# A hybrid mLSTM and GLA decoder step: three column tiles at the head, constants and state traffic on GpSimd's queue, gate rows spread by DMA

## The chip, the cores and the metric

The kernel runs on one core of one Trainium2 chip. The metric is the device time of one execution in microseconds (us). The engines are TensorE (PE; PEld is its weight load), VectorE (DVE), ScalarE (ACT), GpSimd (POOL) and SyncE (SP). SP only issues DMAs here; POOL issues DMAs and does a little arithmetic.

## The reference

One decoder layer is computed for 256 prompt positions and 8 single-token samples, so every matrix product has 264 columns on the moving side (T = 264).

```python
p = x @ w_in                                   # 2048 -> 12312 columns, split into 13 segments
qk = silu(causal_conv(p.qk)); q, k = split(qk) # mLSTM branch
h = mlstm(q, k, v, itil, logf, C, n, m)        # chunkwise, running-max stabiliser m
ya = headnorm(h) * sigmoid(p.o) * silu(p.z)
o = gla(gq, gk, gv, logsigmoid(p.g @ w_gate_up + b) / 16, S)
yb = rmsnorm(o) * silu(p.bz)
merged = sigmoid(p.ga) * (ya @ w_pa) + sigmoid(p.gb) * (yb @ w_pb)
out = layernorm(ALPHA * x + merged @ w_out)
```

Outputs are the new activations of prompt and samples and the new states (C, n, m, conv rows, S) of both. All is float32.

## The kernel before

**Tiles of columns.** `units()` lists 129 column tiles of 128 outputs in a fixed order: 16 qk, one small tile (the gates), 8 av, 4 bq, 4 bk, 8 bv, 16 ao and az, 8 bz, 32 ga and gb, 16 pab, 16 out. For each tile `parts` (L212) runs 16 k slices. A float32 product is made of three fp32r matmuls: weights are split into `hi` (ACT, L203) and `lo` (DVE, L204), x into `xh` and `xl` (`split`, L208), and the slices give hi*xh (L223), hi*xl (L224) and lo*xh (L227). Weights come in pieces of 8 slices, 512 KB each (`load_raw`, L169, on SP's queue), four raw buffers, five buffers each of `hi` and `lo`. So TensorE eats a piece in 24 matmuls.

**Head.** Two tiles (HU = 2) run together at the start, by quarters of x: a quarter of x (528 KB), then a 256 KB weight piece for each of the two tiles, and so on (L1110 to L1118). Behind it come the constants par and cst on SP (L1122, L1123), and six more at tile 4 (L1148).

**Side work.** The rest is written as generators, which `pump` advances by a budget after each tile. PE's order is that of the program (`MANUAL`); DVE, ACT, POOL and SP are ordered by the framework's scheduler when the kernel is built, and each runs its queue strictly in that order. The side work touched here:
- `g_gates` (L280): rows m and u (16 x 264) are split into fp32r halves and spread over 128 partitions by matmuls with a selector `selr`: eight for `dmx` (L377, L378) and, in `g_a_prompt`, four for each head (L423).
- `g_a_decode` (L492): the samples' mLSTM states, 16 chunks `cch` of 512 KB. A chunk is loaded (L526), scaled by ACT (L555), updated by DVE (L571, L573) and stored by POOL (L564). Rows `kb` and `qb` are spread by DMA through `spread_rows` (L486). Loads and spreads go on SP's queue, stores on POOL's.
- `g_gla_prompt` (L678): seven levels of a block recursion; at levels 0 to 4 each of 8 pairs of head and half takes two matmuls with 64 columns (L707) and one masked copy (L730).
- `g_gla_decode` (L771): 8 state chunks `sch` (L778) and the spread rows `ga`, `gk`, `gq` on SP's queue, stores `sS` on POOL's.
- `g_ln_rows` (L940): four loads for the final norm, on SP's queue.

Of the kernel before, what the change touches and what calls it, by code (L numbers as in the profile page):

```python
# [13 lines left out]
F32 = mybir.dt.float32  # L14
# [7 lines left out]
L = 256  # L22
# [3 lines left out]
H = 4  # L26
# [21 lines left out]
HU = 2  # L48
# [35 lines left out]
def body(ctx, tc, xT, wbig, wsmall, par, cmask, lmask, sel, rowc, gate, wgu, cT, sT, nst, cst, lnr,  # L84
# [57 lines left out]
    one_c = const.tile([128, 1], F32, name="one_c")  # L142

# [13 lines left out]
    pieces = [(u, k, KH, u) for k in range(0, KT, KH) for u in range(HU)]  # L157
# [28 lines left out]
    def cast_piece():  # L186
        i = nxt["cast"]
        while nxt["dma"] <= i:
            load_raw()
        n, k, m, bi = pieces[i]  # L190
        nxt["cast"] += 1
        r = raws.pop(i)
        h = whi_p.tile([128, KR, 128], F32R, tag="hi", name="hi")[:, 0:m]
        if bi is None:
            w = SMALL
            A.copy(out=h[:, :, 0:w], in_=r)
            V.tensor_tensor(out=h[:, :, w:2 * w], in0=r, in1=f(h[:, :, 0:w]), op=ALU.subtract)
            for q in range(m):
                his[n, k + q] = h[:, q, 0:2 * w]
            return  # L200
        lo = wlo_p.tile([128, KR, 128], F32R, tag="lo", name="lo")[:, 0:m]
        with tc.high_priority(offset=PRIO):
            A.copy(out=h, in_=r)  # L203
            V.tensor_tensor(out=lo, in0=r, in1=f(h), op=ALU.subtract)  # L204
        for q in range(m):
            his[n, k + q], los[n, k + q] = h[:, q], lo[:, q]
# [5 lines left out]
    def parts(n, k0, k1, rhs, base=0):  # L212

        small = UN[n][0] == "small"
        m = 2 * SMALL if small else 128
        ps = ps_m.tile([128, 512], F32, tag="mm", name="mm")
        out = ps[0:m, 0:T]
        for k in range(k0, k1):
# [8 lines left out]
            PE.matmul(out, lhsT=los[n, k], rhs=rh, start=False, stop=(k == k1 - 1))  # L227
# [9 lines left out]
    st, sel_t = {}, {}  # L237
# [41 lines left out]

    def g_gates(ps):  # L280
# [36 lines left out]
        gr = lambda n: tmp.tile([16, T], F32R, tag="t1", name=n, bufs=T1_BUFS)  # L317
        mh_, ml_, uh, ul = gr("mhi"), gr("mlo"), gr("uhi"), gr("ulo")
        selr = t4([16, 8, 128], "selr", F32R)
        A.copy(out=selr, in_=sel_t["sel"])  # L320
# [13 lines left out]
        split(mh_, ml_, m)  # L334
        split(uh[:, 0:L], ul[:, 0:L], u[:, 0:L])
        st.update(uh=uh, ul=ul, selr=selr)
# [4 lines left out]
        for w, src in ((0, r), (1, wk)):  # L341
            for s in range(2):
                o = w * 32 + s * 16
                PE.transpose(out=pt[:, o:o + 16], in_=src[:, s * 128:(s + 1) * 128], identity=ident[0:16, 0:16])
        dm = one.tile([16, H, NB], F32, tag="dm", name="dm")
# [26 lines left out]
        em = t4([128, H, T], "dmx")  # L372
        st["dmx"] = em
        for hh in (0, 2):
            for h in (hh, hh + 1):
                pp = side_ps()[:, 0:T]
                PE.matmul(pp, lhsT=selr[:, h, :], rhs=mh_, start=True, stop=False)  # L377
                PE.matmul(pp, lhsT=selr[:, h, :], rhs=ml_, start=False, stop=True)  # L378
                A.activation(out=em[:, h, :], in_=pp, func=AF.Exp, scale=-1.0)
            yield 1.0  # L380
# [27 lines left out]
    def g_a_prompt():  # L408
        qT, kT, vt = st["qT"], st["kT"], st["avt"]
        uh, ul, selr, rw, dmx = st["uh"], st["ul"], st["selr"], st["rw"], st["dmx"]  # L410
# [4 lines left out]
        def s1(h):  # L415
            S, U = side_ps(), side_ps()
            Us = U[:, 0:L], U[:, L:2 * L]
            for t0, n, o, s0 in ((0, 256, 0, 0), (128, 128, 256, 128)):
                for d in range(2):
                    PE.matmul(S[:, o:o + n], lhsT=kT.t(2 * h + d)[:, s0:s0 + 128], rhs=qT.t(2 * h + d)[:, t0:t0 + n],  # L420
                              start=(d == 0), stop=(d == 1))
                for ur in (uh, ul):
                    PE.matmul(Us[s0 // 128][:, 0:L], lhsT=selr[:, (s0 // 128) * 4 + h, :], rhs=ur[:, 0:L],  # L423
                              start=(ur is uh), stop=(ur is ul))
            E = tmp.tile([128, 384], F32, tag="E", name="E")
            for s, o, n in ((0, 0, 256), (1, 256, 128)):
                V.scalar_tensor_tensor(out=E[:, o:o + n], in0=Us[s][:, L - n:L], scalar=rw[:, 0, s, h:h + 1],
                                       in1=cm_sb[:, 0:n], op0=ALU.add, op1=ALU.min)
# [57 lines left out]
    def spread_rows(dst, src):  # L486

        n = src.shape[0] * src.shape[1]
        nc.sync.dma_start(out=dst.rearrange("p b d -> p (b d)"),  # L489
                          in_=src.rearrange("r d -> (r d)").unsqueeze(0).to_broadcast([128, n]))  # L490

    def g_a_decode():  # L492
# [14 lines left out]
        nc.sync.dma_start(out=nr, in_=nst)  # L507
# [3 lines left out]
        for x, src in enumerate((kr, qr)):  # L511
            nc.sync.dma_start(out=kq_d[x], in_=src)
# [149 lines left out]
    def g_gla_rows():  # L662
# [11 lines left out]
        nc.sync.dma_start(out=rows_d, in_=rows)  # L674
# [3 lines left out]
    def g_gla_prompt():  # L678
# [19 lines left out]
        for l in range(7):  # L698
            hs = 1 << l
            pl = side3(8, 64)  # L700
            for hf in range(2):
                for h in range(H):
                    for s0, n0, w in {32: ((0, 0, 32), (64, 32, 32)), 64: ((0, 0, 64),)}.get(hs, ((0, 0, 64), (64, 0, 64))):
                        m = min(hs, 64) if hs >= 32 else 64
                        rhs = Q[:, h, hf * 128:hf * 128 + 128].rearrange("p (n two s) -> p n two s", two=2, s=hs)[
                            :, n0 // hs:(n0 + w) // hs, 1, :]
                        PE.matmul(pl[s0:s0 + m, 4 * hf + h, n0:n0 + w].rearrange("p (n s) -> p n s", s=hs),  # L707
                                  lhsT=K[:, h, hf * 128 + s0:hf * 128 + s0 + m], rhs=rhs, start=True, stop=True)
# [11 lines left out]
            av = am.rearrange("p a (n two s) -> p a n two s", two=2, s=hs)[:, :, :, 1, :]  # L720
# [5 lines left out]
            if hs == 64:  # L726
# [3 lines left out]
            V.copy_predicated(out=av, mask=lm_sb[:, l, :].rearrange("p (n s) -> p n s", s=hs).unsqueeze(1).to_broadcast(  # L730
                [128, 8, 64 // hs, hs]), data=pl.rearrange("p a (n s) -> p a n s", s=hs))
# [39 lines left out]
    def g_gla_decode():  # L771
# [168 lines left out]
    def g_ln_rows():  # L940
# [3 lines left out]
        for hf in range(2):  # L944
            gf, hi = t4([128, 1024], "lgf"), t4([128, 1024], "lgh", F32R)
            gg = t4([128, 1024], "lgg", F32R)
            nc.sync.dma_start(out=gf, in_=lnr[:, hf * 1024:hf * 1024 + 1024])
# [4 lines left out]
            nc.sync.dma_start(out=bb, in_=lnr[64:65, hf * 1024:hf * 1024 + 1024].to_broadcast([128, 1024]))  # L952
# [150 lines left out]
    with tc.manual_schedule(engines=MANUAL):  # L1103
# [3 lines left out]
        V.memset(one_c, 1.0)  # L1107
        first = [parts(u, 0, 16, x_rhs) for u in range(HU)]
        head = {}
        for i in range(4):  # L1110
            xr = t4([128, 4, T], "xr")
            nc.sync.dma_start(out=xr, in_=xT[:, 4 * i:4 * i + 4, :])
            while nxt["dma"] < HU * (i + 1):
                load_raw()
            split(x_hi[i], x_lo[i], xr)
            for u in range(HU):
                cast_piece()
                head[u] = next(first[u])  # L1118
        for u in range(HU):
            for _ in first[u]:  # L1120
                pass
        nc.sync.dma_start(out=par_sb, in_=par)  # L1122
        nc.sync.dma_start(out=cst_sb, in_=cst)  # L1123
        for n, (kind, j) in enumerate(UN):
# [15 lines left out]
            else:  # L1140
# [3 lines left out]
                if n == 4:  # L1144
                    V.tensor_copy(out=im_sb, in_=ident)
                    sel_t["sel"] = t4([16, 8, 128], "sel_sb")
                    for dst, src in ((gate_sb, gate), (wgu_sb, wgu), (sel_t["sel"], sel), (rc_sb, rowc), (cm_sb, cmask), (lm_sb, lmask)):
                        nc.sync.dma_start(out=dst, in_=src)  # L1148
# [41 lines left out]
def _layout(v):  # L1190
# [51 lines left out]
    sel = np.zeros((16, 8, 128), np.float32)  # L1242
    for st in range(2):
        for h in range(4):
            for p in range(128):
                sel[(2 * st + p // 64) * 4 + h, st * 4 + h, p] = 1.0
    d["sel"] = sel
# [63 lines left out]
```

## Time and profile before

| | us |
|---|---|
| three runs, median (lowest to highest) | 845.92 (845.65 to 849.77) |
| the profiled execution, its own time | 848.47 |
| its span, first to last instruction | 846.7 |
| PE busy | 826.7 (98%) |
| DVE busy | 591.4 (70%) |
| ACT busy | 451.4 (53%) |
| POOL busy | 45.1 (5%) |

The profiled execution's time lies 1.8 us above its span. Busy times are sums of instruction spans; matmuls overlap, so 98% does not yet mean that the array never idles. Windows count how many instructions touch a stretch, so a matmul on an edge counts on both sides. The column of PEclk is the granted clock in a share of 2.4 GHz (0.50 is 1.2 GHz).

### The profile page before, as it was taken

The numbers are of one execution on the slowest core, as the hardware profiler recorded it, in microseconds if no ns is written. First come the engines' busy times: TensorE is split into PE (matmuls) and PEld (weight loads), VectorE is DVE, ScalarE is ACT, GpSimd is POOL, SyncE is SP. The second block draws the span as 40 slices with busy tenths as digits, with TensorE's granted clock in tenths as the row PEclk, the third lists the DMA queues.
The fourth block names the chain that finished last, engine by engine and source line by source line (L and its number), as shares of the span: only waits on it lengthen the run. The fifth ranks groups of instructions, "written<-read, shape, count | busy, mean of one in ns | idle before, by whom it ended". The sixth has DMA issues, their size and how long they took to land.

```text
span 846.7 us, 16717 instructions
## 1 busy us (share of the span) xinstructions
PE 826.7 (98%) x6773; PEld 813.3 (96%) x6773; DVE 591.4 (70%) x964; ACT 451.4 (53%) x706; POOL 45.1 (5%) x75
## 2 busy tenths in 40 slices
PE   6999999999999999999999998999999999999996
PEld 6999999999899999999999998999999999999995
DVE  6877668545658788757579979994445766666962
ACT  5655457545445653555467747764444444444633
POOL 0000000000001000001000000310000000000410
PEclk9999999999999999999999998999999999999998
DMA  8765565558586985678687799756555555576513
GB/s 318 246 203 181 159 188 171 165 163 262 214 284 225 381 292 189 198 262 312 203 300 243 231 335 329 240 171 203 184 178 184 185 177 177 185 248 214 176 49 103
DMA packets 54766, 184.76 MB, mean 218 GB/s; under 512 B 8209, under 2 KB 9153, under 8 KB 54689
## 3 DMA queue, kind: packets, MB, share of 16 engines
q1 hardware_dynamic: 50560, 169.28, 61.3%
q0 software_dynamic: 4128, 14.42, 4.3%
q8 instruction: 53, 0.87, 0.4%
q14 instruction: 25, 0.20, 0.1%
HBM read 166.98 MB, written 16.69 MB: 217 GB/s over the span
## 4 chain that ended last, share of the span: by engine, by line
PE 81%; DMA 7%; DVE 6%; ACT 2%; issue 2%; SPq 1%; ACTq 0%; POOLq 0%; POOL 0%; DVEq 0%
PE mm L223 25%; PE mm L224 25%; PE mm L227 24%; DMA raw<-wbig 4%; DMA cch<-cT 4%; DVE lo L204 2%; ACT hi L203 1%; DVE scr L573 1%; PE sd L707 1%; PE sd L464 1%; DVE cch L571 1%; ACT cch L555 1%; PE sd L754 0%; SPq L489 0%; PE sd L420 0%
## 5 line engine op out<-in xcount | busy, mean ns | idle before, releaser
L223 PE MATMUL mm<-xh,hi 128*128 128x264 f32 x1552 | 447.2, 289 | 10.2 <-ACT hi L203 9.8
L224 PE MATMUL mm<-xl,hi 128*128 128x264 f32 x1552 | 441.2, 285 | 0.0
L227 PE MATMUL mm<-xh,lo 128*128 128x264 f32 x1536 | 437.2, 285 | 0.5 <-DVE lo L204 0.5
L203 ACT CAST hi<-raw 128x1024 fp32r<-128x1024 f32 (+1 forms) x260 | 267.9, 1034 | 279.5 <-PE mm L224 245.1
L204 DVE TENSOR_TENSOR lo<-raw,hi 128x1024 fp32r<-128x1024 f32 (+1 forms) x260 | 314.9, 1214 | 144.2 <-ACT hi L203 142.0
L223 PEld LDWEIGHTS mm<-xh,hi 128*128 128x128 f32 x1552 | 294.0, 189 | 12.5 <-ACT hi L203 10.0
L224 PEld LDWEIGHTS mm<-xl,hi 128*128 128x128 f32 x1552 | 294.2, 190 | 0.3
L227 PEld LDWEIGHTS mm<-xh,lo 128*128 128x128 f32 x1536 | 290.1, 189 | 1.0 <-DVE lo L204 1.0
L223 PE MATMUL mm<-mh,hi 128*128 128x264 f32 x256 | 72.9, 285 | 0.0
L224 PE MATMUL mm<-ml,hi 128*128 128x264 f32 x256 | 72.7, 284 | 0.0
L227 PE MATMUL mm<-mh,lo 128*128 128x264 f32 x256 | 72.4, 283 | 0.0
L555 ACT ACTIVATE cch<-cch,decb 128x256 f32<-128x256 f32 x64 | 28.0, 500 | 38.6 <-DMA cch<-cT 38.6
L571 DVE SCALAR_TENSOR_TENSOR cch<-kb,avd,cch 128x256 f32<-128x256 f32 x64 | 29.0, 479 | 27.8 <-ACT cch L555 27.8
L227 PEld LDWEIGHTS mm<-mh,lo 128*128 128x128 f32 x256 | 48.2, 188 | 0.0
L223 PEld LDWEIGHTS mm<-mh,hi 128*128 128x128 f32 x256 | 48.1, 188 | 0.0
L224 PEld LDWEIGHTS mm<-ml,hi 128*128 128x128 f32 x256 | 48.1, 188 | 0.0
L224 PE MATMUL mm<-ybl,hi 128*128 128x264 f32 x128 | 36.4, 284 | 0.0
L227 PE MATMUL mm<-yah,lo 128*128 128x264 f32 x128 | 36.4, 284 | 0.0
L223 PE MATMUL mm<-ybh,hi 128*128 128x264 f32 x128 | 36.4, 284 | 0.0
L224 PE MATMUL mm<-yal,hi 128*128 128x264 f32 x128 | 36.2, 283 | 0.0
L227 PE MATMUL mm<-ybh,lo 128*128 128x264 f32 x128 | 36.2, 283 | 0.0
L223 PE MATMUL mm<-yah,hi 128*128 128x264 f32 x128 | 36.2, 282 | 0.0
(323 smaller groups left out, 820.1 us busy)
## 6 DMA issues: line engine op xcount, KB each, us to landing
raw<-wbig SPq DMA_DIRECT2D x252, 512.0 KB, 4.7
cch<-cT SPq DMA_DIRECT2D x16, 512.0 KB, 8.6
sC<-cch POOLq DMA_DIRECT2D x16, 512.0 KB, 5.8
kb<-kq_d SPq DMA_DIRECT2D x8, 512.0 KB, 7.2
qb<-kq_d SPq DMA_DIRECT2D x8, 512.0 KB, 8.8
sch<-sT SPq DMA_DIRECT2D x8, 512.0 KB, 7.6
sS<-sch POOLq DMA_DIRECT2D x8, 512.0 KB, 6.7
xr<-xT SPq DMA_DIRECT2D x4, 528.0 KB, 7.1
```

Of the source, the lines that this page charges most:

```text
L203: A.copy(out=h, in_=r)
L204: V.tensor_tensor(out=lo, in0=r, in1=f(h), op=ALU.subtract)
L223: PE.matmul(out, lhsT=wh, rhs=rh, start=(k == k0), stop=False)
L224: PE.matmul(out, lhsT=wh, rhs=rl, start=False, stop=small and k == k1 - 1)
L227: PE.matmul(out, lhsT=los[n, k], rhs=rh, start=False, stop=(k == k1 - 1))
L464: PE.matmul(CN[:, 0:VC], lhsT=kw[:, s, d * 128:d * 128 + 128], rhs=vt[h // 2][:, s, h % 2, :], start=(s == 0), stop=(s == 1))
L555: A.activation(out=c[:, b, :], in_=c[:, b, :], func=AF.Copy, scale=decb[:, h, b0 + b:b0 + b + 1])
L571: V.scalar_tensor_tensor(out=c[:, b, :], in0=kb[:, b, :], scalar=avd[:, 2 * h + e, b0 + b:b0 + b + 1], in1=c[:, b, :], op0=ALU.mult, op1=A ...
L573: V.scalar_tensor_tensor(out=scr2, in0=c[:, b, :], scalar=1.0, in1=qb[:, b, :], op0=ALU.mult, op1=ALU.mult, accum_out=nd[:, L + b0 + b:L + ...
L707: PE.matmul(pl[s0:s0 + m, 4 * hf + h, n0:n0 + w].rearrange("p (n s) -> p n s", s=hs), lhsT=K[:, h, hf * 128 + s0:hf * 128 + s0 + m], rhs=r ...
```

## The change

- **Head.** Three tiles (HU = 3) by halves of x, weight pieces of the full 512 KB. SP issues x quarter 0, piece, x quarter 1, two pieces, x quarters 2 and 3, piece. x quarters 0 and 1 and the first piece are split in halves. For the first tile's first eight slices the lo matmuls come four slices at a time behind the others. Fifteen plain float32 matmuls of `ones` by `ones` (WARM) stand ahead of all. ACT, DVE and POOL follow the written order in this part.
- **Constants.** Seven loads go out on POOL's queue, behind a copy of one column of x's last quarter (`gate_mark`). The selector `sel` is gone.
- **Spread rows.** u and m are written to DRAM and spread by five DMAs with a broadcast source (`dmx`, and `ub` in four pieces); the 24 selector matmuls go. One Exp over 1056 columns replaces four over 264.
- **GLA.** At levels 0 to 4 each matmul takes 32 columns instead of 64, and each masked copy becomes two of half the partitions and half the columns.
- **Queues.** Every load, spread and small store of the side work moves from SP's queue to POOL's. SP holds x, the weights and the final outputs.

```diff
-HU = 2
+HU = 3
+WARM = 15
...
-    pieces = [(u, k, KH, u) for k in range(0, KT, KH) for u in range(HU)]
+    pieces = [(u, k, KR, u) for k in range(0, KT, KR) for u in range(HU)]
...
+            late.append((los[n, k], rh))
+            if n == 0 and k < KR and k % KH != KH - 1:
+                continue
+            for i, (wl, rh) in enumerate(late):
+                PE.matmul(out, lhsT=wl, rhs=rh, start=False, stop=(k == k1 - 1 and i == len(late) - 1))
+            late.clear()
...
+    def spread_rows(dst, src):
+
+        n = src.shape[0] * src.shape[1]
+        G.dma_start(out=dst.rearrange("p b d -> p (b d)"),
+                    in_=src.rearrange("r d -> (r d)").unsqueeze(0).to_broadcast([dst.shape[0], n]))
...
-        split(mh_, ml_, m)
-        split(uh[:, 0:L], ul[:, 0:L], u[:, 0:L])
+        m_d, u_d = dram.tile([H, T], F32, name="m_d"), dram.tile([16, L], F32, name="u_d")
+        G.dma_start(out=m_d, in_=m[0:H])
+        G.dma_start(out=u_d, in_=u[:, 0:L])
...
+        em, ub = t4([128, H, T], "dmx"), [t4([128, H, L], "ub") for _ in range(2)]
+        spread_rows(em, m_d)
+        for s in range(2):
+            for q in range(2):
+                spread_rows(ub[s][q * 64:q * 64 + 64], u_d[(2 * s + q) * H:(2 * s + q) * H + H])
...
-                for ur in (uh, ul):
-                    PE.matmul(Us[s0 // 128][:, 0:L], lhsT=selr[:, (s0 // 128) * 4 + h, :], rhs=ur[:, 0:L],
-                              start=(ur is uh), stop=(ur is ul))
...
-                nc.sync.dma_start(out=c, in_=cT[i])
+                G.dma_start(out=c, in_=cT[i])
...
-                    for s0, n0, w in {32: ((0, 0, 32), (64, 32, 32)), 64: ((0, 0, 64),)}.get(hs, ((0, 0, 64), (64, 0, 64))):
+                    for s0, n0, w in ((0, 0, 64),) if hs == 64 else ((0, 0, 32), (64, 32, 32)):
...
-                nc.sync.dma_start(out=c, in_=sT[i])
+                G.dma_start(out=c, in_=sT[i])
...
+        warm = side_ps()
+        for _ in range(WARM):
+            PE.matmul(warm[:, 0:128], lhsT=ones, rhs=ones, start=True, stop=True)
...
+        load_x(0)
+        load_raw()
+        load_x(1)
+        load_raw()
+        load_raw()
+        load_x(2)
+        load_x(3)
+        load_raw()
+        with tc.manual_schedule(engines={mybir.EngineType.Activation, mybir.EngineType.DVE, mybir.EngineType.Pool}):
+
+            G.tensor_copy(out=gate_mark, in_=xr[3][:, 3, T - 1:T])
+            for dst, src in ((par_sb, par), (cst_sb, cst), (gate_sb, gate), (wgu_sb, wgu), (rc_sb, rowc), (cm_sb, cmask),
+                             (lm_sb, lmask)):
+                G.dma_start(out=dst, in_=src)
+            split_x(0, 2)
+            cast_piece()
+            split_x(1, 2)
+            for u in range(HU):
+                head[u] = next(first[u])
+                if u:
+                    cast_piece()
+                lay_by(u)
+            split_x(2, 4)
+            split_x(3, 4)
+            for u in range(HU):
+                cast_piece()
+                lay_by(u)
```

How the order moves, at three places. First DVE in the head, before, from the last quarter of x (`xl3`) on; `lo` is a weight piece, `im_sb` the identity as a mask, `dtap`, `ct0` and `co` the preparation of the convolution:

```order
L210 TENSOR_TENSOR xl3_103<-xr_205,xh3_99 128x1056
L204 TENSOR_TENSOR lo_213<-raw_207,hi_212 128x512
L204 TENSOR_TENSOR lo_229<-raw_207,hi_228 128x512
L244 TENSOR_TENSOR dtap_289<-cst_sb_90,par_sb_84 128x128
L246 TENSOR_TENSOR ct0_288<-cst_sb_90,par_sb_84 128x128
L249 COPY co_295<-cst_sb_90 128x16x16
```

and in the changed kernel:

```order
L214 TENSOR_TENSOR xl3_104<-xr_130,xh3_100 128x1056
L1179 CAST im_sb_87<-par_sb_84 128x128
L208 TENSOR_TENSOR lo_255<-raw_141,hi_254 128x1024
L254 TENSOR_TENSOR dtap_356<-cst_sb_90,par_sb_84 128x128
L256 TENSOR_TENSOR ct0_355<-cst_sb_90,par_sb_84 128x128
L259 COPY co_362<-cst_sb_90 128x16x16
L208 TENSOR_TENSOR lo_285<-raw_282,hi_284 128x1024
```

The cast that reads par now stands ahead of the lo part of the first tile's second piece, and the three that read cst ahead of the second tile's.

Second, the GLA decode. SP before, from the second spread on (`raw` are weight pieces):

```order
L489 DMA ga_5825<-rows_d_2815 128x1024
L489 DMA gk_5826<-rows_d_2815 128x1024
L489 DMA gq_5827<-rows_d_2815 128x1024
L778 DMA sch_5831<-sT 128x1024
L778 DMA sch_5916<-sT 128x1024
```

In the changed kernel SP holds one run of 224 weight pieces from the gates to the outputs, and the same loads stand on POOL between the stores `sS`:

```order
L783 DMA sch_5652<-sT 128x1024
L293 DMA ga_5738<-rows_d_2821 128x1024
L293 DMA gk_5739<-rows_d_2821 128x1024
L293 DMA gq_5740<-rows_d_2821 128x1024
L783 DMA sch_5744<-sT 128x1024
L818 DMA sS<-sch_5209 128x1024
L783 DMA sch_5830<-sT 128x1024
L293 DMA ga_5915<-rows_d_2821 128x1024
L818 DMA sS<-sch_5652 128x1024
L293 DMA gk_5916<-rows_d_2821 128x1024
```

No weight piece stands behind a spread any more; a spread stands behind a store.

Third, POOL at the start of the mLSTM decode in the changed kernel, where only the stores stood before:

```order
L527 DMA cch_2536<-cT 128x1024
L565 DMA sC<-cch_2347 128x1024
L483 DMA pC<-pc_2521 128x512
L565 DMA sC<-cch_2441 128x1024
L565 DMA sC<-cch_2536 128x1024
L527 DMA cch_2722<-cT 128x1024
```

The load of the fourth chunk stands behind the store of the third, which is issued when DVE has finished the third.

## Rows read from the trace of the kernel before

**Rows 1.** The page, part 1: busy time, share and instructions of each engine.
```profile
PE 826.7 (98%) x6773; PEld 813.3 (96%) x6773; DVE 591.4 (70%) x964; ACT 451.4 (53%) x706; POOL 45.1 (5%) x75
```
**Rows 2.** Windows at 500 to 518: length, PE, PEld, DVE, ACT, POOL busy (instructions), PEclk, DMA, GB/s.
```profile
500.00:502.00 2.00, 2.00 (x19) 2.00 (x18) 1.97 (x5) 2.00 (x6) 0.53 (x1) 1.00 0.92 225
...
506.00:508.00 2.00, 1.41 (x12) 1.20 (x10) 1.24 (x3) 0.00 (x0) 0.00 (x0) 1.00 1.02 416
508.00:510.00 2.00, 0.00 (x0) 0.00 (x0) 1.27 (x4) 1.09 (x2) 0.00 (x0) 0.96 1.04 422
510.00:512.00 2.00, 1.54 (x5) 1.24 (x6) 2.00 (x3) 1.67 (x4) 0.00 (x0) 0.50 0.91 281
514.00:516.00 2.00, 2.00 (x11) 2.00 (x10) 2.00 (x3) 1.33 (x3) 0.00 (x0) 0.50 0.88 299
516.00:518.00 2.00, 2.00 (x16) 2.00 (x15) 2.00 (x4) 0.00 (x0) 0.00 (x0) 0.83 1.00 377
```
**Rows 3.** Timeline of SP's queue, 483 to 503: start, length, engine, line, operation.
```profile
483.85 2.23 SPq L181 DMA_DIRECT2D raw<-wbig  x2
...
497.53 0.33 SPq L489 DMA_DIRECT2D gk<-rows_d  x1
...
499.90 3.25 SPq L181 DMA_DIRECT2D raw<-wbig  x4
```
**Rows 4.** Timeline of ACT, 497 to 510; in brackets the idle time before and its end.
```profile
497.13 1.05 ACT L203 CAST hi<-raw 128x1024 fp32r<-128x1024 f32 x1 [0.83 <-DMA raw<-wbig]
...
508.91 1.04 ACT L203 CAST hi<-raw 128x1024 fp32r<-128x1024 f32 x1 [6.11 <-DMA raw<-wbig]
```
**Rows 5.** Timeline of PE, the selector matmuls of the first head.
```profile
185.18 0.38 PE L423 MATMUL sd<-uhi,selr 16*128 16x256 f32 x1
...
185.60 0.71 PE L420 MATMUL sd<-qT,kT 128*128 128x128 f32 x4
```
**Rows 6.** Timeline of PE: GLA level 0, level 5, and four plain float32 transposes.
```profile
317.72 1.15 PE L707 MATMUL sd<-gq,gk 128*64 128x64 f32 x32 [1.50 <-DVE gq L714]
...
346.06 0.70 PE L707 MATMUL sd<-gq,gk 128*32 128x32 f32 x32
...
366.38 1.03 PE L745 MATMUL sd<-par_sb,gk 128*128 128x128 f32 x8
```
**Rows 7.** Windows of the head, same columns.
```profile
0.00:10.00 10.00, 2.78 (x11) 2.56 (x12) 3.27 (x8) 5.00 (x6) 0.20 (x4) 1.00 0.81 266
10.00:20.00 10.00, 10.00 (x79) 10.00 (x78) 9.24 (x17) 6.37 (x10) 0.00 (x0) 1.00 1.02 381
20.00:30.00 10.00, 10.00 (x85) 10.00 (x85) 8.07 (x12) 7.61 (x10) 0.00 (x0) 1.00 0.73 227
```
**Rows 8.** Timeline of ACT in the head: first weights, x quarters 1 and 3.
```profile
6.55 1.31 ACT L203 CAST hi<-raw 128x512 fp32r<-128x512 f32 x2 [1.13 <-DMA raw<-wbig]
8.59 1.07 ACT L209 CAST xh<-xr 128x1056 fp32r<-128x1056 f32 x1 [0.73 <-DMA xr<-xT]
...
14.23 1.08 ACT L209 CAST xh<-xr 128x1056 fp32r<-128x1056 f32 x1 [0.63 <-DMA xr<-xT]
```
**Rows 9.** DMA issues: transfer, queue, count, KB each, median us from issue to landing.
```profile
sC<-cch POOLq DMA_DIRECT2D x16, 512.0 KB, 5.8
...
pconv<-co POOLq DMA_DIRECT2D x1, 216.0 KB, 4.9
...
cm_sb<-cmask SPq DMA_DIRECT2D x1, 128.0 KB, 2.7
```
**Rows 10.** Timeline of DVE: a whole lo piece.
```profile
19.19 1.22 DVE L204 TENSOR_TENSOR lo<-raw,hi 128x1024 fp32r<-128x1024 f32 x1
```
**Rows 11.** Timeline of ACT in the mLSTM decode: two neighbouring hi pieces.
```profile
209.20 1.05 ACT L203 CAST hi<-raw 128x1024 fp32r<-128x1024 f32 x1 [0.79 <-ACT E L429]
217.00 0.91 ACT L555 ACTIVATE cch<-cch,decb 128x256 f32<-128x256 f32 x2 [6.74 <-DMA cch<-cT]
217.81 1.04 ACT L203 CAST hi<-raw 128x1024 fp32r<-128x1024 f32 x1
```

More of the change, by code (lines that the diff above doesn't have):

```diff
@@ L83, in body @@
 @with_exitstack
-def body(ctx, tc, xT, wbig, wsmall, par, cmask, lmask, sel, rowc, gate, wgu, cT, sT, nst, cst, lnr,
+def body(ctx, tc, xT, wbig, wsmall, par, cmask, lmask, rowc, gate, wgu, cT, sT, nst, cst, lnr,
          y, yd, pC, pn, pm, pconv, pS, sC, sn, sm, sS):
@@ L142, in body @@
     one_c = const.tile([128, 1], F32, name="one_c")
+    gate_mark = const.tile([128, 1], F32, name="gate_mark")
     def P(name, j=0, n=None):
@@ L202, in cast_piece @@
         with tc.high_priority(offset=PRIO):
-            A.copy(out=h, in_=r)
-            V.tensor_tensor(out=lo, in0=r, in1=f(h), op=ALU.subtract)
+            for q in range(0, m, KH if i == 0 else m):
+                c = slice(q, q + (KH if i == 0 else m))
+                A.copy(out=h[:, c], in_=r[:, c])
+                V.tensor_tensor(out=lo[:, c], in0=r[:, c], in1=f(h[:, c]), op=ALU.subtract)
         for q in range(m):
@@ L217, in parts @@
         out = ps[0:m, 0:T]
+        late = []
         for k in range(k0, k1):
@@ L371, in g_gates @@
         yield 1.5
[L372 to L380, printed above, removed]
+        A.activation(out=em, in_=em, func=AF.Exp, scale=-1.0)
+        yield 1.0
         st["num"], st["oT"] = Tiles("num"), Tiles("oT")
@@ L506, in g_a_decode @@
             PE.transpose(out=pt[0:64, x * 128:x * 128 + 128], in_=qkd[:, x].rearrange("p h b t -> p (h b t)"), identity=ident)
-        nc.sync.dma_start(out=nr, in_=nst)
+        G.dma_start(out=nr, in_=nst)
         A.copy(out=qr, in_=pt[0:64, 0:128])
@@ L511, in g_a_decode @@
         for x, src in enumerate((kr, qr)):
-            nc.sync.dma_start(out=kq_d[x], in_=src)
+            G.dma_start(out=kq_d[x], in_=src)
         yield 0.5
@@ L673, in g_gla_rows @@
         rows_d = dram.tile([96, 128], F32, name="rows_d")
-        nc.sync.dma_start(out=rows_d, in_=rows)
+        G.dma_start(out=rows_d, in_=rows)
         st["rows"] = rows_d
@@ L729, in g_gla_prompt @@
                 break
-            V.copy_predicated(out=av, mask=lm_sb[:, l, :].rearrange("p (n s) -> p n s", s=hs).unsqueeze(1).to_broadcast(
-                [128, 8, 64 // hs, hs]), data=pl.rearrange("p a (n s) -> p a n s", s=hs))
+            for s0, n0 in ((0, 0), (64, 32)):
+                r = slice(s0, s0 + 64)
+                V.copy_predicated(
+                    out=am[r, :, s0:s0 + 64].rearrange("p a (n two s) -> p a n two s", two=2, s=hs)[:, :, :, 1, :],
+                    mask=lm_sb[r, l, n0:n0 + 32].rearrange("p (n s) -> p n s", s=hs).unsqueeze(1).to_broadcast(
+                        [64, 8, 32 // hs, hs]),
+                    data=pl[r, :, n0:n0 + 32].rearrange("p a (n s) -> p a n s", s=hs))
             yield 3.0
@@ L946, in g_ln_rows @@
             gg = t4([128, 1024], "lgg", F32R)
-            nc.sync.dma_start(out=gf, in_=lnr[:, hf * 1024:hf * 1024 + 1024])
+            G.dma_start(out=gf, in_=lnr[:, hf * 1024:hf * 1024 + 1024])
             A.copy(out=hi, in_=gf)
@@ L1107, in body, with load_x, split_x, lay_by @@
         V.memset(one_c, 1.0)
+        warm = side_ps()
+        for _ in range(WARM):
+            PE.matmul(warm[:, 0:128], lhsT=ones, rhs=ones, start=True, stop=True)
         first = [parts(u, 0, 16, x_rhs) for u in range(HU)]
[L1109 to L1115, printed above, removed]
+        head, xr = {}, [t4([128, 4, T], "xr") for _ in range(4)]
+        def load_x(i):
+            nc.sync.dma_start(out=xr[i], in_=xT[:, 4 * i:4 * i + 4, :])
+        def split_x(i, step):
+            for k in range(0, 4, step):
+                split(x_hi[i][:, k:k + step], x_lo[i][:, k:k + step], xr[i][:, k:k + step])
+        def lay_by(n):
+            for _ in range(KR // KH):
+                next(first[n], None)
+        load_x(0)
[21 more added lines that the diff above has]
+            split_x(3, 4)
             for u in range(HU):
                 cast_piece()
[L1118 to L1123, printed above, removed]
+                lay_by(u)
         for n, (kind, j) in enumerate(UN):
@@ L1241, in _layout @@
     d["lmask"] = lm
[L1242 to L1247, printed above, removed]
     rc = np.zeros((64, 108), np.float32)
@@ L1301 @@
     args = []
-    for name in ("xT", "wbig", "wsmall", "par", "cmask", "lmask", "sel", "rowc", "gate", "wgu", "cT", "sT", "nst", "cst", "lnr"):
+    for name in ("xT", "wbig", "wsmall", "par", "cmask", "lmask", "rowc", "gate", "wgu", "cT", "sT", "nst", "cst", "lnr"):
         a = arrays[name]
```

26 lines of the change are left out of this document (6 added, 20 removed).

## The prediction

> **What bounds the kernel now.** I read the page first: TensorE is busy 98% of the span [rows 1], so a microsecond counts only if TensorE issues less or waits less. The windows come next, since matmuls overlap and hide short gaps: at full rate 10 us touch 85 matmuls [rows 7], a pitch of 10 / 85 = 0.118 us, so a weight piece of 24 matmuls is eaten in 2.8 us. Against that rate two stretches fall short.
>
> The first is the head. Until 20.0 us TensorE has issued 11 + 79 = 90 matmuls [rows 7], worth 90 x 0.118 = 10.6 us: 9.4 us are lost. Of these 10 - 2.78 = 7.2 lie before the first matmul and 2.2 behind it, when the array starts slow.
>
> The second is at 506 to 518. A full window of 2 us touches 19 matmuls; the five windows shown and the one at 512, which reads like that at 514, touch 12, 0, 5, 11, 11 and 16, so 59 are missing: 59 x 2 / 19 = 6.2 us. Half of it is a wait, the rest the granted clock, 0.50 from 510 to 516 after the array had stood for more than 2 us [rows 2]. The chain behind it: ACT casts a piece at 497.13 and the next at 508.91, having waited 6.11 us for the weights [rows 4]. The weights were late because SP runs in order: it issues two pieces at 483.85, then stands before a spread of `gk` until 497.53, and issues the next piece at 499.90 [rows 3].
>
> All times are set against the profiled execution's own 848.47 us, which is 2.55 above the median of the three runs, 845.92. If the median run stalls less at 506, part of that gain is already in it; the changed kernel's own time is not moved by this.
>
> **The change part by part.**
>
> *TensorE work removed.* The selector matmuls of u: a pair costs 185.60 - 185.18 = 0.42 us [rows 5], switch to and from plain float32 included; 8 pairs give 3.4. The eight for m stand among main matmuls, 8 x 0.118 = 0.9. GLA: a level of 16 matmuls with 64 columns lasts 1.15 us, the level with 32 columns 0.70 [rows 6]; five levels give 5 x 0.45 = 2.25. That form also has 32 output rows where the new one has 64, so the saving may be nothing: its bounds are 0 and 2.25, and I take the upper, as the column count is what the rows vary most clearly. Sum 6.6, bounds 4.3 and 6.6. These matmuls stand in PE's own order, so nothing hides them.
>
> *SP holds weights alone.* The stall at 506 had one cause, a spread ahead of the weights, and that order is gone: 6.2 us. Bounds 0 (another stall in its place) and 6.2.
>
> *The loads on POOL.* About 70 transfers change the queue. A POOL transfer of 512 KB lands in 5.8 us median [rows 9], and its issue takes 0.53 of POOL [rows 2], which is 95% idle [rows 1]: the issue itself costs nothing. The price is order: loads stand behind stores that wait for DVE. What absorbs a late load is the stock of cast weights. ACT casts at 209.20 and next at 217.81, 8.6 us later, after waiting 6.74 for a state chunk [rows 11], and TensorE did not stop; at 11.8 us between casts [rows 4] it did. A load issued late by one store has about that much room, so I take 0; the other end is one stall of 6.2.
>
> *u and m by DMA.* Two small stores, then five broadcast loads of 1.6 MB in all. From u to the last piece the path is a store (at most 4.9, the nearest POOL row), five or six issues of 0.53 and a landing of 5.8 [rows 2, 9], some 13 us. DVE reads `ub` four lo pieces after u, 4 x 2.8 = 11.3 us later. A wait of 2 us on DVE, and about as much on ACT before the Exp, is inside the 8.6 us of above: 0.
>
> *Warm-up matmuls.* A plain float32 matmul of 128 columns is two records; eight records take at most 1.03 us [rows 6], 0.26 each matmul at 2.4 GHz, about twice that at 1.2. Fifteen need 3.9 to 7.7 us. They run in the 7.2 us in which TensorE has nothing to do; at the slow end they delay the first real matmul by up to 1.5, at the other they give back the 2.2 us of the slow start.
>
> *Head by halves.* The same bytes stand before x quarter 1 as before, so it lands near 8.59 and x quarter 3 near 14.23 [rows 8]. The first piece is now 512 KB, both halves of what was there at 6.55 to 7.2: the first matmul moves by 0 to 0.6. After 12 matmuls TensorE waits for half of quarter 1 (8.59 + 0.5 for ACT + 0.6 for DVE = 9.7), and after 24 for the second tile's lo piece. By my count the 72 matmuls on the first half of x end near 17.8, where the old order had as many: what the clock gives, these waits take. Net 0, bounds -1 and +2.
>
> *The constants.* Here a new wait stands on the path. DVE casts `im_sb` from par before it makes the lo part of the first tile's second piece. par is issued after x quarter 3: 14.23, then 0.7 for POOL's copy and issue, then a landing between 2.7 (a load of 128 KB) and 4.9 (216 KB by POOL) [rows 9], say 3.5: 18.4. The cast and the piece (0.2 + 1.22 [rows 10]) end at 19.9, and TensorE needs it at 17.8 + 0.2 = 18.0: it waits 1.9 us. Bounds 0 and 3.3; above some 2.5 the clock falls too, as at 508 [rows 2], for another 3. I take -2 for the head in all, bounds +2 and -6.
>
> **Sum:** 6.6 + 6.2 - 2.0 = 10.8; 848.47 - 10.8 = 837.7, say 838.
>
> **The rivals.**
>
> *The head keeps its gain (par early, warm clock).* For: at 18 us the DMA engines are less crowded than at 12. Against: par cannot leave before x has landed. The head then gives +2 in place of -2: 833.7.
>
> *The stall moves to POOL's queue.* One state chunk or spread comes late behind a store, ACT or DVE stand before it with casts behind them, and one stall of 6.2 us takes the place of that at 506. For: the fourth chunk's load stands behind the store of the third. Against: the 8.6 us of room. 837.7 + 6.2 = 843.9.
>
> *The narrower GLA matmul is no shorter.* Then the change doesn't do there what it says: 837.7 + 2.25 = 840.
>
> *Slower: POOL's order stalls the mLSTM decode again and again.* Sixteen chunks pass through one queue, each load behind a store that waits for DVE, and DVE waits for the load. It decides from the point at which the gap between two hi casts goes past some 9 to 12 us [rows 4, 11], that is when issue and landing together take that long after the chunk before. Each stall costs 6.2 with its slow clock; the 12.4 us from 837.7 up to 850.15 (0.5% above the median) are two stalls, and with two to three it is 850 to 856, say 853. Against: 16 stores by POOL leave in 0.5 us each while DVE is busy 1.97 of 2.00 us [rows 2], so nothing holds the queue but waits of its own. The Trainium skill, "SBUF — State Buffer", section "SBUF: two separate sides", speaks against this change: while DVE runs an operation in a two-port mode, GpSimd cannot write descriptors, so DMAs from its queue stand, and loads should stay on SP or ACT. By that rule each issue would stretch to the DVE operation beside it; the 0.53 in that window does not bear it out, though the loads of this change may meet other operations than the stores did. The chance below counts it in.
>
> **How the numbers follow.** Forecast 838 with 0.45; the head's gain 833.7 with 0.17; the stall on POOL 843.9 with 0.22; GLA no shorter 840 with 0.05; slower 853 with 0.11. The range 832 to 846 takes in all but the last and the edges of the others. A measurement of this kernel can tell 0.5%, 4.2 us, from no change: faster means below 841.7, slower above 850.15. Below 841.7 lie the forecast, the first and the third rival and a little of the second: 0.68. Between: 0.22. Above: most of the last: 0.10.
>
> **What would show it.** In the windows: from 20 to 30 us no fewer than 85 matmuls, and about 2 us of PE idle near 18 with DVE's `im_sb` as releaser and a DMA of par behind it. At 500 to 520 19 matmuls in each 2 us and a granted clock of 1.00. No selector matmuls between the plain ones of a head, and five GLA levels of 0.7 us. SP never waits on anything but freed buffers. The prediction is wrong if PE waits for casts in the decode (190 to 400), if the first real matmul comes after 8.5, or if the GLA levels still take 1.1.

## The result: 1.35% slower

Four runs of the changed kernel take 858.32 us in the median (856.9 to 859.72), four of the kernel before 846.02 (845.65 to 849.77): a ratio of 1.0135, 95% interval 1.0102 to 1.0168. The forecast was 838, its range ended at 846. The profiled execution took 858.42 us with a span of 856.6, 9.9 longer than that of before.

### The profile page after: what moved, and what is told of

It reads as the page before. It is cut to its first block, busy times and chain, and to the rows that moved or that the text cites. A ratio compares the mean times of both kernels' runs of the same rounds, so it can differ in the third digit from the quotient of the medians.

```text
span 856.6 us, 16743 instructions
## 1 busy us (share of the span) xinstructions
PE 826.0 (96%) x6779; PEld 815.2 (95%) x6779; DVE 593.7 (69%) x966; ACT 451.6 (53%) x699; POOL 81.2 (9%) x150
## 4 chain that ended last, share of the span: by engine, by line
PE 82%; DMA 6%; DVE 6%; issue 2%; ACT 2%; POOL 1%; SPq 0%; ACTq 0%; POOLq 0%; DVEq 0%
PE mm L228 25%; PE mm L229 25%; PE mm L236 25%; DMA cch<-cT 4%; DVE lo L208 2%; DMA xr<-xT 1%; PE sd L708 1%; DVE scr L574 1%; ACT hi L207 1%; DMA par_sb<-par 1%; DVE gpr L814 1%; PE sd L430 1%; DVE cch L572 1%; PE sd L471 1%; DVE sch L813 0%
## 5 line engine op out<-in xcount | busy, mean ns | idle before, releaser
L556 ACT ACTIVATE cch<-cch,decb 128x256 f32<-128x256 f32 x64 | 27.8, 500 | 23.9 <-DMA cch<-cT 23.9
```

The lines of the kernel that those rows point to most:

```text
L556: A.activation(out=c[:, b, :], in_=c[:, b, :], func=AF.Copy, scale=decb[:, h, b0 + b:b0 + b + 1])
```

## The profile after

Part 1 of the page of the changed kernel, to be set against [rows 1]:

```profile
PE 826.0 (96%) x6779; PEld 815.2 (95%) x6779; DVE 593.7 (69%) x966; ACT 451.6 (53%) x699; POOL 81.2 (9%) x150
```

Only POOL has clearly more to do (it issues 109 DMAs instead of 35, and is still 91% idle), and TensorE is idle for longer. The longest waits of PE (engine, tile, line, awaited; us in total, times, longest) name four places:

```profile
PE sd L708 <- DVE gq L715: 6.7, 1, 6.7
PE mm L236 <- DVE lo L208: 3.7, 2, 3.4
PE sd L834 <- DVE ns L829: 2.6, 2, 2.1
PE sd L411 <- ACT vT L404: 1.4, 1, 1.4
```

To see what each place costs in the end, I took from PE's timeline when the k-th matmul of the column tiles starts (6,176 in either kernel, counted from 0, in the same order but for the head) and subtracted:

| k | 200 | 1800 | 2000 | 2400 | 3400 | 3600 | 4000 | 6000 |
|---|---|---|---|---|---|---|---|---|
| before, start in us | 34.2 | 264.5 | 289.7 | 348.7 | 485.0 | 514.5 | 565.6 | 808.4 |
| after minus before | +5.7 | -1.0 | +0.6 | +8.0 | +8.0 | +2.6 | +4.8 | +4.8 |

So: the head loses 5.7. From there to the 1800th matmul 6.7 are won, all at the places where the selector matmuls stood; 1.6 of them go again at the 2000th, where TensorE waits for a copy of ACT (`vT`). At the second GLA level, between 2000 and 2400, 7.4 are lost. The stop near 506 is gone (5.4 won), 2.2 are lost behind it, at the norm of the GLA output (L834), and the last matmul comes 4.8 later than before. The remaining 5.1 lie behind it, in the tail.

**Head.** Windows (columns as in [rows 7]; the first contains the 30 records of the plain matmuls) and the timelines of POOL, DVE and PE:

```profile
0.00:10.00 10.00, 7.08 (x43) 6.47 (x43) 3.54 (x9) 4.75 (x7) 0.20 (x4) 1.00 0.82 273
10.00:20.00 10.00, 8.04 (x61) 7.54 (x61) 5.69 (x6) 7.41 (x7) 4.91 (x8) 1.00 0.97 372
20.00:30.00 10.00, 8.12 (x45) 8.12 (x46) 7.95 (x15) 3.50 (x4) 0.00 (x0) 0.66 0.61 190
```
```profile
14.09 1.06 POOL L1141 COPY gate_mark<-xr 128x1 f32<-128x1 f32 x1 [13.64 <-DMA xr<-xT]
15.09 0.73 POOL L1144 DMA_DIRECT2D par_sb<-par  x1
...
13.84 2.59 DVE L214 TENSOR_TENSOR xl<-xr,xh 128x1056 fp32r<-128x1056 f32 x2 [0.20 <-ACT xh L213]
20.47 0.23 DVE L1179 CAST im_sb<-par_sb 128x128 int32<-128x128 f32 x1 [4.03 <-DMA par_sb<-par]
20.61 1.22 DVE L208 TENSOR_TENSOR lo<-raw,hi 128x1024 fp32r<-128x1024 f32 x1
...
21.88 0.59 PE L236 MATMUL mm<-xh,lo 128*128 128x264 f32 x1 [3.45 <-DVE lo L208]
```

From 20 to 30 us 45 matmuls stand where [rows 7] has 85. DVE stands 4.03 us before the cast of `im_sb`; par, issued at 15.09, is there 5.4 us later. The lo piece behind the cast lets TensorE go on at 21.88, after 3.45 us, with a granted clock of 0.50 from 21.0 to 27.8.

**Second GLA level.** POOL, ACT, DVE and PE, one fence from four timelines in order of cause:

```profile
295.58 0.53 POOL L565 DMA_DIRECT2D sC<-cch  x1 [3.23 <-DVE cch L572]
296.10 0.53 POOL L293 DMA_DIRECT2D kb<-kq_d  x1
296.62 0.53 POOL L293 DMA_DIRECT2D qb<-kq_d  x1
297.15 1.04 POOL L527 DMA_DIRECT2D cch<-cT  x2
...
309.71 2.21 ACT L556 ACTIVATE cch<-cch,decb 128x256 f32<-128x256 f32 x5 [12.10 <-DMA cch<-cT]
...
310.25 0.89 DVE L572 SCALAR_TENSOR_TENSOR cch<-kb,avd,cch 128x256 f32<-128x256 f32 x2 [6.19 <-ACT cch L556]
...
323.02 0.69 DVE L715 TENSOR_TENSOR gq<-gq,gE 128x512 f32<-128x512 f32 x1
...
323.85 1.92 PE L708 MATMUL sd<-gq,gk 128*64 128x32 f32 x32 [6.73 <-DVE gq L715]
```

POOL waits 3.23 us for DVE before a store; behind it stand two spreads and two chunks, which go out within 1.6 us of each other and land 8.4, 10.5, 12.5 and 13.7 us after their issue. The first of the chunks is there at 309.7. Until then ACT casts nothing for 12.1 us, and DVE stands 6.2; from 312.9 on it works without a pause, but the product that the GLA level needs comes at 323.02. The product is 6.1 us later than in the kernel before (there it ended at 317.6), while TensorE is 0.9 later at the same matmul: here the side work is late, not TensorE early. (The level at 317.72 in [rows 6] is this one; the rows call it level 0, but it is the second of the five, level 1.) TensorE stood 6.7 us and comes back at a granted clock of 0.50: this level takes 1.92 us, the level ahead of it

```profile
309.69 1.13 PE L708 MATMUL sd<-gq,gk 128*64 128x32 f32 x32
```

1.13. That is next to the 1.15 of a level with 64 columns in [rows 6]: the narrower form saves 0.02.

ACT's waits for the chunks, before and after (us in total, times, longest):

```profile
ACT cch L555 <- DMA cch<-cT: 38.6, 13, 6.7
```
```profile
ACT cch L556 <- DMA cch<-cT: 23.9, 6, 12.1
```

The sum fell in the slower kernel; the stop of TensorE goes with the longest one.

**Tail.** The last instructions of POOL, of the change and of before (line, engine, operation, count: min/median/max ns, first and last start):

```profile
L1332 POOLq DRAIN  x3: 46/98/9427, 846.4 to 856.4; - x3
```
```profile
L1307 POOLq DRAIN  x3: 40/93/3394, 841.6 to 846.4; - x3
```

POOL's queue is drained from 846.4 on, for 9.43 us; before, for 3.39. The last output was there at 850.5, and the program ends 0.8 us behind the drain. Before, the drain ended at 845.0, ahead of the last output at 845.7.

## Experiments

Behind each time stand, in brackets, its ratio to runs of the kernel before from the same comparison and the 95% interval of that ratio. In those comparisons the kernel before had medians of 846.77 to 847.25.

### What POOL's last drain counts

`d_tiny` adds 74 transfers to the kernel before, `d_fat` 9 with nearly as many pieces as the change adds packets:

```diff
+            if 20 <= n < 94:
+                G.dma_start(out=note_d[n - 20:n - 19], in_=cm_sb[0:1, 0:16])
```
```diff
+            if 20 <= n < 92 and n % 8 == 4:
+                G.dma_start(out=note_d[n // 8 - 2][:, :, 0:16], in_=cm_sb[:, 0:128].rearrange("p (a b) -> p a b", b=16))
```

> The kernel before with 74 more DMAs on POOL, each of 16 words, all issued in the first 70 us. They ask what the last drain of POOL counts. Per transfer: 74 x 0.082 = 6.0 us more, a drain of 9.4 and a time of 852. Per packet (0.67 ns each, 1,184 more at most): a drain of 4.2 and 846.8. Only what is recent or still under way: a drain of 3.4 and 846.

> The kernel before with 9 more DMAs on POOL early in the program, each of 1,024 pieces of 64 bytes: nearly as many packets more (9,216) as the change brings (9,024), with few transfers. Per packet: a drain of 9.5 us. Per transfer: 4.1. Only what is recent: 3.4. The rest of the time may be longer by the small packets beside the weights, so the drain alone is read here.

The drains of `d_tiny` and of `d_fat`:

```profile
L1310 POOLq DRAIN  x3: 40/240/9442, 849.8 to 860.2; - x3
```
```profile
L1310 POOLq DRAIN  x3: 40/102/4129, 841.1 to 846.0; - x3
```

9.44 and 4.13: per transfer, as forecast to 0.05 us, however small the transfer and however long ago. All sixteen kernels of this study lie on 0.54 + 0.0816 us for each DMA on POOL. What shows of it is the stretch from the start of the last matmul of the tiles to the end of the span:

| DMAs on POOL | 35 | 42 to 44 | 54 | 102 | 109 |
|---|---|---|---|---|---|
| drain, us | 3.4 | 4.0 to 4.1 | 4.9 | 8.9 | 9.4 |
| last matmul to end, us | 17.0 to 17.2 | 17.1 to 17.4 | 17.7 | 21.6 | 22.2 to 22.6 |

Up to 44 the drain is hidden by the landing of the last output. `d_tiny` took 864.06 (1.0213, 1.0171 to 1.0255), some 11 us more than its tail explains: its small transfers went out from 41 us on, more slowly than I had thought, and beside them the weights landed in 10.5 us (median) between 60 and 122. That is not explained further.

### The loads back on SP

```diff
-                G.dma_start(out=c, in_=cT[i])
+                nc.sync.dma_start(out=c, in_=cT[i])
```

and so in every line of the side work that loads, spreads or stores a row to be spread.

> The changed kernel with the loads, spreads and small stores of the side work back on SP (the constants and the stores of the states stay on POOL). Theory: POOL's queue costs two things, the stop of 6.7 us at 317 with its slow clock (2.2 more, 8.9 in all) and the long last drain. POOL then issues 42 DMAs in place of 109; between 35 DMAs (3.39 us) and 109 (9.43) that gives a drain of 4.0, so 5.4 less. The stall behind a spread of `gk` comes back with 6.2. So 858.3 - 8.9 - 5.4 + 6.2 = 850. Rival A: the stop at 317 comes from the order of the GLA work on DVE and not from the queue; then it stays and the time is 859. Rival B: the drain has nothing to do with POOL's DMAs and stays at 9.4: 855.

852.29 (1.006, 1.0035 to 1.0085), 6 below the change. Drain 3.96 us. PE's longest waits (the third is that of the head):

```profile
PE sd L834 <- DVE ns L829: 4.0, 1, 4.0
PE sd L708 <- DVE gq L715: 3.6, 1, 3.6
PE mm L236 <- DVE lo L208: 3.2, 2, 3.0
```

The drain went as expected, and the tail is 4.8 shorter: that is most of the 6. The stop at the GLA level was halved, not gone (its product comes at 318.6 instead of 323.7), and that at the norm (L834) grew: TensorE, held up less at one place, stands longer at the next, and its last matmul comes only 1.3 earlier than in the change. The stop near 506, expected back with 6.2, is not in this profile.

### The head

`h_prep_last` writes the cast and the preparation of the convolution behind the head's six pieces (and no longer at tiles 0 and 4); `b_head_old` takes the part *Head* and the part *Constants* of the change back.

```diff
             for u in range(HU):
                 cast_piece()
                 lay_by(u)
+            V.tensor_copy(out=im_sb, in_=ident)
+            g_conv_prep()
```

> The changed kernel with the cast of `im_sb` and the preparation of the convolution written behind the six weight pieces of the head; everything else is as in the change. Theory: the DVE queue alone makes the head slow, because `im_sb` waits for par (20.47 us) ahead of a lo piece. In the changed kernel's windows 59 matmuls are missing from 18 to 28 us, 59 x 2 / 19 = 6.2 us, so this kernel takes 858.3 - 6.2 = 852 and no matmul waits more than 0.5 us between 14 and 28. Rival: the weights of the second half of x come late in any case and take the place of par; then a wait of 2 us or more on ACT's cast stands near 20 us and the time stays at 856 to 858.

858.54 (1.0136, 1.01 to 1.0172): nothing won. The wait for lo is gone, and another is there. A wait of PE, then DVE and ACT in time:

```profile
PE mm L228 <- ACT co L273: 3.8, 1, 3.8
```
```profile
25.77 1.23 DVE L208 TENSOR_TENSOR lo<-raw,hi 128x1024 fp32r<-128x1024 f32 x1 [2.93 <-ACT hi L207]
...
29.98 0.29 DVE L259 COPY co<-cst_sb 128x256 f32<-128x256 f32 x1
...
30.69 0.17 ACT L273 COPY co<-mm 128x11 f32<-128x11 f32 x1 [0.74 <-DVE cacc L270]
```

The preparation, now strewn among lo pieces that wait for weights (2.93), ends at 30.3. Until 30.9 ACT hasn't emptied the first tile's buffer of sums, and with three head tiles none of the three buffers (`ps_m`, L97) is left for the fourth tile. Neither theory had this: par was there at 20.0, but the preparation had now been put behind the lo pieces, and it became what TensorE waits for in the end. Three tiles with par ahead of x were not tried.

> The changed kernel with its head undone (two tiles by quarters of x, no plain matmuls ahead, constants on SP behind the weights), all else as in the change. Theory: the new head costs what the windows of 0 to 30 us show, 56 matmuls fewer than before at 2 / 19 us each, 5.9 us; without the seven constants POOL issues 102 DMAs and the last drain falls by 7 x 0.082 = 0.6. So 858.3 - 6.5 = 852, with the stop near 317 and a drain of 8.9 still there. Rival: the head is made up for later, since another wait comes at its place; then 857 to 858.

858.96 (1.0131, 1.0087 to 1.0176). The progress of the matmuls is within 0.4 us of that of before at the 200th, so 5.3 us are won against the change. Of these 3.7 are left at the 2000th matmul and 2.4 at the 2400th; at the 4000th this kernel is 1.6 behind the change. PE's longest waits behind the head:

```profile
PE sd L700 <- DVE gq L707: 6.7, 1, 6.7
PE sd L826 <- DVE ns L821: 4.2, 1, 4.2
```

The rival held: TensorE came earlier and stood for it later. This made a new theory. At two places, the second GLA level and the norm of the GLA output, TensorE has an appointment with the side work on ACT and DVE. What is won ahead of an appointment that TensorE already reaches too early is lost there, with the slow clock on top. In this run it was lost at three: 1.5 us at the copy `vT` (L403), then at the level and the norm.

### Parts of the change alone

`b_um_dma` is the kernel before with the part *Spread rows* of the change. `b_um_gspread` adds the GLA spreads on POOL:

```diff
-                    spread_rows(x, rows[32 * i + 8 * h:32 * i + 8 * h + 8, :])
+                    spread_rows(x, rows[32 * i + 8 * h:32 * i + 8 * h + 8, :], G)
```

> The kernel before with one part of the change: u and m go out and come back spread by seven DMAs on POOL, and the selector matmuls go. Theory: 4.3 us of matmuls less and nothing else, since 42 DMAs on POOL keep the drain at 4.0, still behind the landing of yd: 846.6 - 4.3 = 842. Rival: DVE or ACT stand before the spread rows, and the matmuls saved come back as waits of `sd` on DVE in 180 to 300 us: 845 or more.

847.2 (0.9996, 0.9978 to 1.0015). At the 1800th matmul this kernel is 6.8 us ahead of before, at the 2000th, behind a wait of 1.6 for `vT`, 5.0, and at the 2400th 1.5:

```profile
PE sd L700 <- DVE gq L707: 3.7, 1, 3.7
PE sd L822 <- DVE ns L817: 3.5, 2, 3.1
```

> As the kernel with u and m by DMA, and the twelve spreads ga, gk, gq of the GLA decode on POOL too, so that no weight piece stands behind them. Theory: the stall near 506 goes (6.2 us), 54 DMAs make a drain of 4.9, of which 0.9 shows: 5.3 below the kernel with u and m by DMA, about 837. Rival: the spreads, now behind the stores on POOL, stop DVE and with it TensorE at the same place: no gain, 842 to 844.

846.59 (0.998, 0.9959 to 1.0002), above both the theory and the rival. The stop near 506 is absent, but so it is in the profile of the kernel above, whose GLA spreads are all on SP: it does not belong to every execution. Other profiles with these spreads on SP have 1.3 us there (`b_warm`) or 1.5 (`d_fat`), each in two waits without a fall of the clock.

`b_warm` puts the plain matmuls alone ahead of the kernel before:

```diff
+        warm = side_ps()
+        for _ in range(15):
+            PE.matmul(warm[:, 0:128], lhsT=ones, rhs=ones, start=True, stop=True)
```

> The kernel before with the fifteen plain matmuls ahead of all and nothing else. In the trace of before the first 19 matmuls, from 7.2 to 11.4 us, come 0.22 us apart and then 0.12; in the changed kernel they come 0.12 apart from the first. Theory: 19 x 0.10 = 1.9 us less, 844.7. Rival: the quarters of x come no sooner, so that TensorE only waits longer for them: 846.6.

847.68 (0.9997, 0.9974 to 1.0021). The rival held: at the 200th matmul it is 0.3 us ahead. The matmuls of the tiles come 0.12 us apart from the start wherever they don't wait (before: 0.22 up to 11.4 us), but now they wait for the pieces of the head (1.0 at 7.7 us, 0.2 at 8.4 and at 12.0).

### Moving the appointments

If TensorE comes too early, its order can be changed instead. Two yields move the GLA level and the norm one tile, 5.8 us, later in TensorE's order:

```diff
             yield 3.0
+            if l == 0:
+                yield 3.0
...
             if h % 2:
                 yield 1.2
+        yield 2.8
```

> The kernel before with the same two places one tile later. In its profile TensorE waits 1.5 us at the first and nothing at the second, in two other kernels with its side work 0.9 to 2.6 and 1.8 to 3.7. Theory: 2 to 4 us less, 843 to 845. Rival: no change, 847, as DVE and ACT are only busier later.

842.07 (0.9953, 0.9937 to 0.9969): a gain of 4.0 by the ratio, the upper end of the forecast 2 to 4. All that PE waits for, beside 7.1 us at the start, is

```profile
PE mm L227 <- DVE lo L204: 1.0, 2, 0.8
```

> The kernel before with u and m by DMA, the fifteen plain matmuls ahead, and the two places one tile later. Theory: what u and m (4.3 to 5 us in the progress of the matmuls up to 290 us) and the plain matmuls (0.3 to 1.9) give was lost only because TensorE came earlier to places at which it has to wait: with these moved it is kept, 847 - 4.5 - 0.5 - 2 = 840. Rival: the waits move on, and the time stays at 845 to 847.

838.79 (0.9916, 0.9895 to 0.9938). The selector matmuls that gave nothing by themselves now give, with the plain matmuls, 3.3 us.

> As the last one, and the twelve spreads ga, gk, gq on POOL, with 54 DMAs there and a drain of 4.9 us, of which 0.9 shows. Theory: no weight piece stands behind a spread, so the stop near 506, which shows in some executions (2.6 us and its slow clock) and less in others (0.8), goes: 840 - 3 + 0.9 = 838. Rival: the stop was not regular enough to count, and the drain adds its 0.9: 841.

838.17 (0.991, 0.9889 to 0.993), with a tail of 17.7 us: the 0.9 for the drain came out as 0.5. It is the lowest median of the study, but not told apart from the one above, so neither theory nor rival is decided for the spreads.

> The changed kernel with two places of the side work one tile (48 matmuls, 5.8 us) later in TensorE's order: the second GLA level, at which it stands 6.7 us, and the norm of the GLA output, at which it stands 2.6. Theory: TensorE stands there because the side work on ACT and DVE, held up by the chunk that lands at 309.7, is not ready, and one tile of other matmuls covers it: 5.8 of the 6.7 us, the slow clock behind (2.2) and the 2.6 us go, 858.3 - 10.6 = 848. Rival: the side work is the bound of the whole stretch, and the next level waits instead: 855 or more.

859.65 (1.0151, 1.0128 to 1.0173): nothing, as the rival said. TensorE now stands at the third level, and at a lo piece near 519:

```profile
PE mm L236 <- DVE lo L208: 8.1, 6, 3.1
PE sd L708 <- DVE gq L715: 6.1, 2, 5.3
```
```profile
505.58 0.53 POOL L293 DMA_DIRECT2D gq<-rows_d  x1 [3.19 <-DMA sS<-sch]
506.10 0.53 POOL L785 DMA_DIRECT2D sch<-sT  x1
...
516.66 0.69 DVE L814 TENSOR_TENSOR sch<-sch,ga 128x512 f32<-128x512 f32 x1 [7.49 <-DMA sch<-sT]
```

POOL's queue holds the GLA chunk back until a spread ahead of it has found a free buffer (3.19 us, behind a store), and DVE then stands 7.5 us, with lo pieces behind it. Is it this order, or the side work itself?

> The changed kernel with both edits at once: the loads and spreads back on SP, and the two places one tile later. Each alone gave 852.3 and 859.7. Theory: it is the order on POOL's queue that moved the stop from one GLA level to the next; with the loads on SP the side work is late by less than a tile, the 3.6 and 4.0 us that TensorE still stood in the kernel with the loads on SP go, and some 2 us of slow clock: 852.3 - 9.6 = 843. Rival: the side work is late by itself (new spreads, split masks), and the stop moves on as it did with the loads on POOL: 850 or more.

844.72 (0.9961, 0.9932 to 0.999). Each of the two edits alone left the kernel at 852.3 and 859.7; together they take 13.6 us off. Neither of the two appointments holds TensorE any more; the stop near 506 is there in the profiled execution (847.56, one of the slower ones of ten), as SP has the spreads again:

```profile
PE mm L228 <- ACT hi L207: 3.7, 2, 3.5
```

So what kept the side work late was that its loads stood on POOL's queue: with them there the two yields won nothing, without them 7.6 (852.29 to 844.72). That it is their order on the queue is read from the fences and not separated by a run; slower transfers as such it hardly is, as a chunk's median landing is 8.6 us on SP before and 8.9 on POOL in the change.

> As the last one, with the head of before (two tiles by quarters, constants on SP, no plain matmuls). With loads on POOL the old head gave nothing back (858.96 against 858.32), as TensorE only waited longer later. Theory: with no stops left behind it, the head's loss of 4.2 us at the 200th matmul, as the kernel with the loads on SP has it, shows in the end: 4 us below the last one, 839. Rival: the rest absorbs it again: the same time within 1 us.

840.01 (0.9904, 0.987 to 0.9938), 4.7 below. With little left to absorb it, the loss at the head (4.2 at the 200th matmul) shows whole, as far as the intervals tell.

## Why the prediction was wrong

*The loads on POOL.* This step failed, and twice. First, "the issue itself costs nothing" looked at the 0.53 us of an issue [rows 2], and so it stayed, 0.53 in the fences above also beside a busy DVE; the longest issue of the change took 0.73. A stretching of the issues by DVE, as the prediction worked it out from the Trainium skill ("SBUF — State Buffer", "SBUF: two separate sides"), shows nowhere; whether an operation of the two-port kind ran beside them no run here tells. But each DMA on POOL adds 0.082 us to the drain at the end, and 109 of them are past what the last output's landing hides: 5.1 us, a term that the sum lacked and that no rival had. A drain of 3.39 us stood in the trace of before; I had read the profile only up to the last matmul. Second, the room of "8.6 us" was taken from a gap between casts [rows 11], and the landing, 5.8, from the median of a store [rows 9], though the page of the profile of before had the loads themselves, on SP:

```profile
cch<-cT SPq DMA_DIRECT2D x16, 512.0 KB, 8.6
```

Four transfers let go at once by one store landed in up to 13.7 us. And weights were not the stock that ran out: DVE was late with the GLA product.

*Its rivals.* That the stall moves to POOL's queue was given 0.22 and did happen, at one stop of 6.7 us plus some 2 of slow clock. The slower rival named the right queue, but its mechanism, several stalls in the mLSTM decode, is not what came.

*The constants and the head.* Named in the right place (DVE's cast of `im_sb` ahead of lo), and mis-sized: 5.4 us for the landing of par where I took 3.5 (bound 4.9), 1.06 us for a copy of one column where 0.7 stood for copy and issue; TensorE waited 3.45 instead of 1.9, and the clock fell. The 2.5 from which I had it fall is not borne out as a limit: a wait of 2.6 at 510 came with a fall before, one of 2.6 at the GLA level (`b_warm`) and one of 2.7 in the head (the kernel of 844.72) without. The head lost 5.7, beside the forecast 2.0 and its bound of 6.

*TensorE work removed.* That the sum of 6.6 agrees with the 6.7 won by the 1800th matmul is luck. The 4.3 for u and m were too low: 6.6 in the kernel with that part alone, as two pairs taken out of a head shortened its block of side work from 2.98 to 1.79 us, 1.2 where the sum had two times 0.42 [rows 5]. The 2.25 for GLA are not there: 1.13 against 1.15. I took the upper bound because columns were what the rows varied "most clearly", while in [rows 6] columns and output rows vary together; the level with 32 rows is still the only short one.

*SP holds weights alone.* The mechanism was right, the place is clean in the change (5.4 won). But 6.2 us were priced from one execution, itself 2.55 above the median, and the profiles of kernels that keep the spreads on SP show from nothing to 4.0 us of waiting there. What a median run loses is probably less than one such stop; only single profiles tell it.

*The sum.* From 837.7 to the 858.4 of the profiled execution it is 20.7 us: 5.1 of tail, 7.4 at the second GLA level, 2.2 at the norm, 1.6 at `vT`, 3.7 more at the head, 0.8 less at 506, and 0.1 more won on the selector matmuls than the 6.6. The first four, 16.3 us, were put at nothing. Under the three waits lies one error: gains were added up as if nothing met TensorE on the way. It meets the side work, and waits where it comes earlier (as with u and m alone) or where the side work comes later (as in the change). The 1.50 us wait in [rows 6], the clearest mark of an appointment in the trace of before, was quoted and not used. In the change, undoing the head gave 0; with the loads on SP and the appointments moved it gave 4.7.

## What to carry to other kernels

Where one engine's order is fixed and the others feed it, look for places where it waits even a little for side work: a saving ahead of such a place gave little or nothing here until the place was moved. Two yields that moved them took 4.0 us off the kernel before by the ratio, and 7.1 together with two parts of the change that had given nothing alone; the whole change was meant to bring 7.9 below the median. Read the trace to the end of the span, and count the DMAs on GpSimd's queue: they are paid again at the end, each alike, once they outlast the last output. Price a stall from several executions, and a queue from what one release lets go at once, not from the median of single transfers.

## What was not expected of the hardware

- POOL's last drain takes 0.54 + 0.0816 us for each DMA that POOL has issued in the whole program, from 64 bytes to 528 KB; 74 transfers of 64 bytes issued more than 700 us earlier made it 6.05 us longer.
- A GLA level of 16 matmuls with 64 output rows takes nearly as long with 32 columns as with 64 (1.13 and 1.15 us).
- Small transfers beside the weights go with late weights: 52 transfers of 64 bytes went out between 60 and 122 us, and the weight pieces landed in 10.5 us there (median), against 4.5 in the same window of the kernel before. That the one makes the other was not tried by itself.
- Executions of one kernel differ by more than the first three runs showed: before lay between 843.5 and 853.1 us in the later comparisons, so that single parts had to be read by ratios with their intervals.

What stays open: whether the chunk at 297 landed late because four transfers share POOL's queue, or because weights refill at the same time. The core's DMA engines had a busy share of 0.89 to 1.08 in every window of 2 us from 296 to 308, and weight pieces issued in that time took 9.2 to 9.8 us, too, so transfers of both queues were slow while the DMA engines were full; that speaks for the load as a whole, but does not separate the two. A kernel with the spreads on one queue and the chunks on another would tell; it was not tried.
